# The first feed-forward step's way down as seven block products for eight, and the gate and up sums made by one transfer and three VectorE additions in both steps

## The chip, the cores and the metric

The kernel runs on one core of one Trainium2 chip. The metric is the device time of one execution in microseconds (us), as the median of several runs. TensorE (PE) multiplies, VectorE (DVE) and ScalarE (ACT) do the element-wise work, GpSimd (POOL) and SyncE (SP) issue transfers, POOL also some small copies. Every engine works through its own queue in order; the program that builds the kernel may draw an instruction ahead of its written place if what it needs is there, and fixes the order of each queue before the run.

## The reference

One layer of a decoder stack works on 512 prompt rows and 64 sample rows (8 sequences of 8) with the same weights, 1024 channels wide:

```python
x = x + 0.5 * swiglu(rmsnorm(x, ffn1_norm), ffn1_w_gate, ffn1_w_up, ffn1_w_down)
...  # mixer: RG-LRU heads and pooling heads between w_in and w_out
...  # cross attention over 256 memory rows, 4 heads
x = x + 0.5 * swiglu(rmsnorm(x, ffn2_norm), ffn2_w_gate, ffn2_w_up, ffn2_w_down)
y = rmsnorm(x, final_norm)

def swiglu(x, w_gate, w_up, w_down):
    return (silu(x @ w_gate) * (x @ w_up)) @ w_down
```

The hidden width of a feed-forward step is 2816, that is 22 chunks of 128. All arrays are float32.

## The kernel before

`x` lies transposed in SBUF, channels on partitions: 8 tiles of 128 channels by T = 576 rows, the rows in two halves of HT = 288. Every product is done in fp32r with hi and lo parts: `split` (L188 to L193) makes the hi part with a ScalarE cast and the lo part with a VectorE subtraction, and each block product is three matmuls (hi x hi, hi x lo, lo x hi). A panel of weights therefore costs one cast and one subtraction before TensorE can use it. The tiles of hi and lo parts rotate through WSB = 5 buffers (tags `wh`, `wl`), the raw weights through WRB = 4 (tag `wr`).

Both feed-forward steps are one function, `ffn`; the second is called with `fast=True`.

**Gate and up.** The first chunks (STD: 3 in the first step, 2 in the second) are multiplied plainly. For every further chunk, gate and up weights and the two halves of the rows form a 2 x 2 block product, done as seven block products instead of eight. The products are called by their weight operand: 11, E, F, G, 12, H and 22; each is 4 blocks x 3 matmuls = 12 matmuls of 288 columns. The operands of the activations (`n1`, `n2`) are prepared once; the weights of each chunk have to be summed. E, F, G and H are sums or differences of the four weight blocks.

- First step: `load` brings all four blocks by two SP transfers, and `prepare_a` and `prepare_b` make the sums with four VectorE additions of 128x512 (L472, L473, L474, L485).
- Second step: two of the sums come from HBM. During the first step and the mixer, `background` has POOL copy blocks into a scratch array `gsum` and accumulate the others onto them (L173, L176). `load_pairs` fetches them, and `sum_g` (L509, L510) makes the other two on VectorE. `prepare_e`, `prepare_g`, `prepare_h` and `prepare_22` split the pairs.

**Way down.** Its products are `steps` in a queue; `fill()` puts one of them between two products of a chunk.

- First step: plain. Five groups of chunks (FGS = 4, 4, 4, 5, 5). For each group and each of 8 output panels, `down` multiplies the hidden chunks by the panel's weights (tile `pd`, 6 matmuls a chunk), and VectorE adds the result to `x` (L572). The last group runs after the last chunk, and each finished panel goes straight to the mixer's norm (`after(j)`). The hidden chunks are split as they are made (`hh`, `hl`).
- Second step: chunks 0 to 15 form four groups of four, each again a 2 x 2 block product done as seven (`quick`; tiles `d`). `build_a` and `build_b` make the operands from two hidden chunks with four subtractions and five splits (tiles `ph`, `pl`). `ensure` makes the weight operands of one of the 16 down tiles: two sums from `dsum` in HBM (made by `background` like `gsum`), two by VectorE (L657), four splits. Results go to `x` by accumulating POOL transfers (`take`, then L694, L721, L728). Chunks 16 to 21 (PLAIN) go through `down` in groups of two and four; the last group is the tail with the final norm.

A group of seven products has 6 slots: `s11`, `sE`, `sF`, `s12`, `sH`, and `sG` with `s22`. Each block product here is 2 blocks x 3 matmuls = 6 matmuls.

The order of TensorE's instructions is as written (`chain` in `mm`). The place where `background` may issue is tied to the latest matmul. `first` ties the ScalarE casts that are written after it behind a given instruction.

## Time and profile before

| | |
|---|---|
| median of 3 runs | 1133.25 us (1132.85 to 1133.92) |
| the profiled execution | 1133.87 us, of which the span of its instructions is 1132.1 us |
| TensorE busy | 1118.3 us, 8526 instructions |
| VectorE busy | 833.0 us |
| ScalarE busy | 604.0 us |
| POOL busy | 135.0 us |
| first feed-forward step | about 5 to 399 us |
| mixer and output projection | about 399 to 541 us |
| attention | about 541 to 738 us |
| second feed-forward step with the tail | about 739 us to the end |

The page gives busy time by engine, then the chain of work that ended last, then groups of instructions by source line, operation and tile; a group's row ends with its busy time, the mean duration of one in ns, and the idle time of its engine just before it with what ended that. Matmuls overlap, so a single one shows about 295 ns while one starts every 133 ns. Other views list who waited for whom, the transfers with the median time to landing, and the busy time of all engines in given stretches.

### The profile page before, as it was taken

To read this page: it belongs to the slowest core of one execution; us is meant where nothing else is said; L and a number is where in the kernel's file an instruction comes from. 1 tells how busy PE (TensorE), PEld (TensorE's weight loads), DVE (VectorE), ACT (ScalarE), POOL (GpSimd) and SP (SyncE) were. 2 spreads that over 40 slices of the span, in tenths; PEclk is the share of its full clock that TensorE was granted. 3 is DMA by queue.
4 is the path that set the end of the run, shared out by engine and by line. 5 is a ranking of instruction groups with operands and counts; after the bars stand their busy time and mean duration, and the time that the engine had idled before them with its cause. 6 is when DMAs were issued, how large, how long until landed. Compare 5 with 4: busy or idle time off the path is not lost.

```text
span 1132.1 us, 21308 instructions
## 1 busy us (share of the span) xinstructions
PE 1118.3 (99%) x8526; PEld 1101.1 (97%) x8526; DVE 833.0 (74%) x1391; ACT 604.0 (53%) x1047; POOL 135.0 (12%) x177
## 2 busy tenths in 40 slices
PE   9999999999999999999999999999999999999996
PEld 8999999999999999999999889999999999999996
DVE  8887778787775698977733666669878888787644
ACT  8544444444432454875721455446666666666544
POOL 0011111111111033310000000000121111212111
PEclk9999999999999999999999999999999999999998
DMA  9355766576675388642566762223675766766652
GB/s 317 99 146 153 183 168 160 139 170 174 154 181 113 102 234 184 125 153 86 189 207 215 270 229 79 77 79 94 163 171 150 188 161 163 193 164 157 152 118 84
DMA packets 82547, 179.58 MB, mean 159 GB/s; under 512 B 8272, under 2 KB 28752, under 8 KB 82320
## 3 DMA queue, kind: packets, MB, share of 16 engines
q1 hardware_dynamic: 55728, 129.92, 35.6%
q0 software_dynamic: 24064, 45.88, 22.7%
q10 hardware_dynamic: 2656, 2.41, 0.6%
q8 instruction: 67, 1.10, 0.4%
q14 instruction: 32, 0.26, 0.1%
HBM read 156.86 MB, written 34.17 MB: 169 GB/s over the span
## 4 chain that ended last, share of the span: by engine, by line
PE 93%; DVE 3%; DMA 1%; ACT 1%; issue 1%; SPq 0%; DVEq 0%; ACTq 0%
PE pu L140 22%; PE pd L140 15%; PE pc L140 11%; PE d L140 7%; PE pa L140 5%; PE q L140 5%; PE wo L140 5%; PE xo L140 5%; PE pg L140 2%; PE in_l L140 2%; PE in_p L140 2%; PE in_g L140 2%; PE v L1396 2%; PE k L140 2%; PE o L140 1%; PE s L140 1%
## 5 line engine op out<-in xcount | busy, mean ns | idle before, releaser
L140 PE MATMUL pd<-hh,dh 128*128 128x288 f32 x352 | 75.3, 295 | 0.0
L140 PE MATMUL pd<-hl,dh 128*128 128x288 f32 x352 | 75.0, 294 | 0.0
L140 PE MATMUL pd<-hh,dl 128*128 128x288 f32 x352 | 75.0, 294 | 0.0
L188 ACT CAST wh_e<-r 128x1024 fp32r<-128x1024 f32 x39 | 41.0, 1051 | 57.5 <-PE pu L140 22.8
L140 PE MATMUL d<-ph,dh 128*128 128x288 f32 x224 | 66.6, 297 | 0.2 <-ACT add_e L677 0.2
L140 PE MATMUL d<-ph,dl 128*128 128x288 f32 x224 | 66.0, 295 | 0.0
L140 PE MATMUL d<-pl,dh 128*128 128x288 f32 x224 | 65.8, 294 | 0.0
L694 POOL DMA_DIRECT2D x<-add_e x16 | 19.3, 1204 | 380.8 <-ACT dh L188 348.6
L140 PEld LDWEIGHTS pd<-hl,dh 128*128 128x128 f32 x352 | 56.5, 188 | 0.0
L140 PEld LDWEIGHTS pd<-hh,dh 128*128 128x128 f32 x352 | 56.4, 188 | 0.0
L140 PEld LDWEIGHTS pd<-hh,dl 128*128 128x128 f32 x352 | 56.1, 188 | 0.0
L191 DVE TENSOR_TENSOR wl_e<-r,wh_e 128x1024 fp32r<-128x1024 f32 x39 | 47.7, 1222 | 10.5 <-ACT wh_e L188 10.5
L188 ACT CAST wh_g<-r 128x1024 fp32r<-128x1024 f32 x39 | 41.0, 1052 | 22.1 <-DVE r L485 15.1
L191 DVE TENSOR_TENSOR wl_g<-r,wh_g 128x1024 fp32r<-128x1024 f32 x39 | 47.7, 1223 | 5.2 <-ACT wh_g L188 4.1
L188 ACT CAST dh<-wr_d 128x512 fp32r<-128x512 f32 (+2 forms) x50 | 31.0, 619 | 36.0 <-PE pd L140 14.7
L140 PE MATMUL pu<-n1h,wh_a 128*128 128x288 f32 x152 | 45.0, 296 | 0.0
L140 PE MATMUL pu<-n1h,wl_a 128*128 128x288 f32 x152 | 44.9, 295 | 0.0
L140 PE MATMUL pu<-n1l,wh_a 128*128 128x288 f32 x152 | 44.6, 293 | 0.0
L936 ACT ACTIVATE g<-g 128x576 f32<-128x576 f32 x39 | 26.8, 686 | 32.8 <-DVE g L935 32.6
L140 PEld LDWEIGHTS d<-ph,dh 128*128 128x128 f32 x224 | 42.0, 188 | 0.8 <-ACT add_e L677 0.4
L191 DVE TENSOR_TENSOR dl<-td,dh 128x512 fp32r<-128x512 f32 x48 | 33.1, 690 | 12.6 <-ACT dh L188 10.9
L140 PEld LDWEIGHTS d<-pl,dh 128*128 128x128 f32 x224 | 42.2, 188 | 0.0
(570 smaller groups left out, 4250.1 us busy)
## 6 DMA issues: line engine op xcount, KB each, us to landing
gsum<-f_gu POOLq DMA_DIRECT2D x40, 512.0 KB, 8.5
r<-f_gu SPq DMA_DIRECT2D x38, 512.0 KB, 3.9
r<-f_gu SPq DMA_DIRECT2D x60, 256.0 KB, 3.8
x<-add POOLq DMA_DIRECT2D x40, 288.0 KB, 4.3
r<-gsum SPq DMA_DIRECT2D x40, 256.0 KB, 4.0
dsum<-f_d POOLq DMA_DIRECT2D x32, 256.0 KB, 5.6
ck<-ck SPq DMA_DIRECT2D x16, 512.0 KB, 4.4
cv<-cv SPq DMA_DIRECT2D x16, 512.0 KB, 6.9
```

The costliest lines, as they stand in the source:

```text
L140: i = te.matmul(*args, **kw)
L188: i = cast[0] = s.copy(hi, src)
L191: return v.tensor_tensor(out=lo, in0=src, in1=f(hi), op=ALU.subtract)
L694: nc.gpsimd.dma_start(x[:, j:j + 2, HT:], t, accum_op=ALU.add)
L936: s.activation(g, g, AF.Silu, scale=-1.0)
L1396: te.matmul(ps[:, m, :HD], lhsT=lhs[:, kd, ms], rhs=w[wi][:, k, :], start=kd == 0 and i == 0, stop=kd == DC - 1 and i == 2)
```

## The change

The first step's `ffn` now works like the second: `fast` is gone, and both use `quick`, `ensure`, `build_a`, `build_b` and PLAIN for the way down. In the first step the last group (chunks 18 to 21) is still added to `x` by VectorE, panel by panel, for the mixer's norm. The two sums of down weights that the second step takes from `dsum` are made by VectorE in the first (`ensure`, `elif head`).

In both steps `gsum` is gone. A chunk's blocks come by SP transfers (`load_11`, `load_12`, `load_22`). `sum_eh` makes H by one VectorE addition, and E by a POOL transfer from HBM that accumulates onto the raw block; it is written two chunks ahead of use. `prepare_g` makes the other two sums with two VectorE additions. The splits of H/12 and of G/F are written one product later than before, that of 22 one product earlier. The 32 transfers for `dsum` remain and are now issued in the mixer and the output projection. WRB goes from 4 to 6, WSB from 5 to 4. Small things: the constants `ones` and `eps` share a tile, `neg` keeps two gains, the `half` factor is gone (the 0.5 is applied on the way down), and in the last scaling VectorE's first multiply stands ahead of ScalarE's copy of the row factor.

```diff
-WRB, WSB = 4, 5
+WRB, WSB = 6, 4
...
-    nfast = FFC - STD[1]
-    gsum = [scratch.tile([P, 2, KP * P], F32, name=f"gsum{i}") for i in range(nfast)]
     dsum = [scratch.tile([NQ, P, 2, 2 * P], F32, name=f"dsum{i}") for i in range(FAST)]
...
-        def prepare_a(f):
...
-        def prepare_b(f):
...
-        def load_pairs(f):
+        def load_11(f, behind=None):
             if f < FFC:
...
+                raws[f] = [raw_tile("r0")]
+                i = nc.sync.dma_start(raws[f][0], wgu[f - plain, :, 0:2])
+                if behind is not None:
+                    after_(i, behind)
+
+        def load_12(f, behind=None):
+            if f < FFC:
+                raws[f].append(raw_tile("r1"))
+                i = nc.sync.dma_start(raws[f][1][:, 0], wgu[f - plain, :, 2])
+                if behind is not None:
+                    after_(i, behind)
+
+        def sum_eh(f):
+            if f < FFC:
+                r0, r1 = raws[f]
+                v.tensor_add(r1[:, 1], r0[:, 0], r0[:, 1])
+                nc.gpsimd.dma_start(r0[:, 0], wgu[f - plain, :, 3], accum_op=ALU.add)
...
-        def sum_g(f):
+        def prepare_g(f):
             if f < FFC:
                 r0, r1 = raws[f]
                 v.tensor_add(r0[:, 1], r0[:, 1], r0[:, 0])
                 v.tensor_add(r0[:, 0], r0[:, 1], r1[:, 0])
-
-        def prepare_g(f):
-            if f < FFC:
-                W[f]["G"], W[f]["F"] = parts_of(raws[f][0], "g")
+                W[f]["G"], W[f]["F"] = parts_of(r0, "g")
...
-                if k == fg - 1 and fast:
+                if k == fg - 1 and after:
+                    xj = halves(x[:, j, :])
+                    v.scalar_tensor_tensor(out=xj, in0=pd[j][:, :, :HT], scalar=0.5, in1=xj, op0=ALU.mult, op1=ALU.add)
+                    after(j)
+                elif k == fg - 1:
                     add = rows.tile([P, T], F32, tag="sq", name="add")
                     s.activation(halves(add), pd[j][:, :, :HT], AF.Copy, scale=0.5)
                     nc.gpsimd.dma_start(x[:, j, :], add, accum_op=ALU.add)
...
+        def fetch_pair(i):
...
                     if k:
                         v.tensor_add(t[:, k], t[:, k], t[:, k - 1])
+                    elif head:
+                        v.tensor_add(t[:, 3], t[:, 0], t[:, 1])
+                        v.tensor_add(t[:, 0], t[:, 0], draw[i, 0])
                     split(*w, t[:, k:k + 2])
                     if k == 2:
-                        fetch_main(i + 1)
+                        fetch_pair(i + 1)
...
+        if head:
+            ps2 = accumulators(2)
+            w = panel(wstd[2, 0], DC, P, "s", load_behind=squares_in)
+            load_11(plain, squares_in)
+            load_12(plain, squares_in)
+            sum_eh(plain)
+            std(cols(ps2[0]), w, range(DC))
+            load_22(plain)
+            std_out(1, *ps1)
+            n.sums(3, ts[1][:, 1])
+            w = panel(wstd[2, 1], DC, P, "s")
+            first[0] = spread_out
+            prepare_e(plain)
+            std(cols(ps2[1]), w, range(DC))
+            load_11(plain + 1)
+            load_12(plain + 1)
+            std_out(2, *ps2)
+            prepare_g(plain)
+            first[0] = None
...
             product(U, w["11"], n, N11, True)
             s.copy(A, U)
...
+            if f == plain:
+                if not head:
+                    prepare_g(f)
+                load_11(f + 2)
...
             product(C, w["E"], n, T1, True)
             e1 = small_tile("e1")
             s.copy(e1, C)
-            if fast and f == 3:
+            prepare_h(f)
+            load_12(f + 2)
+            if f == plain:
+                sum_eh(f + 1)
+            if f == 3:
                 build_a(0)
                 build_b(0)
             fill()
             if before:
                 finish_chunk(before)
...
+            prepare_e(f + 1)
             fill()
-            if fast and f in range(4, 4 * FAST + 1, 4):
+            if f in range(4, 4 * FAST + 1, 4):
                 quick(f // 4 - 1)
             product(U, w["F"], n, T2, False)
             u2 = small_tile("u2")
             s.copy(u2, U)
-            if fast:
-                sum_g(f + 1)
+            prepare_22(f)
+            load_22(f + 2)
             fill()
             product(C, w["G"], n, N22, False)
...
+            sum_eh(f + 2)
             fill()
...
             product(A, w["12"], n, N21, False)
...
             fill()
             product(U, w["H"], n, T3, False)
...
+            prepare_g(f + 1)
+            load_11(f + 3)
             raw[f] = g
...
-        s.copy(rb, pr)
-        finish(nc.gpsimd, nc.scalar, c0, c1, 6, 8, rb)
         for i in range(3):
             finish(v, nc.sync, c0, c1, 2 * i, 2 * i + 2, pr)
+            if i == 0:
+                s.copy(rb, pr)
+                finish(nc.gpsimd, nc.scalar, c0, c1, 6, 8, rb)
```

More of the change, by code (lines that the diff above doesn't have):

```diff
@@ L798, in ffn @@
         for i in range(3):
-            i = s.copy(r[:, i * third:(i + 1) * third], free[i][:, HT:HT + third])
-        spread_out = i
-        if fast:
-            half = r
-        else:
-            half = fp.tile([P, T], F32, name=f"half_{n.name}")
-            s.activation(half, r, AF.Copy, scale=0.5)
-        std(cols(ps1[1]), w, range(mid, DC))
-        if not fast:
-            group(0)
-        std_out(0, *ps0)
-        if fast:
-            load_pairs(plain)
+            spread_out = s.copy(r[:, i * third:(i + 1) * third], free[i][:, HT:HT + third])
@@ L839, in ffn @@
[L839 to L857 removed]
+        load_22(plain + 1)
@@ L877, in ffn @@
         for f in range(plain, FFC):
-            if not fast and f - g0 == FGS[gi]:
-                g0, gi = f, gi + 1
-                group(gi)
             w = W[f]
@@ L1515, in hybrid_step @@
                 copy()
+                if h == XH - 2:
+                    first[0] = cast[0]
         sample_values(7)
@@ L1524, in hybrid_step @@
         prompt_values(3)
+        first[0] = None
         end("xa")
@@ L1540, in hybrid_step @@
                 n2.sums(j // 2, now["r1"].tile([P, 3, HT], F32, tag="A", bufs=2, name=f"t_n2{j}"))
+    assert not jobs and not added
     end("r2", "r1", "ps")
```

266 lines of the change are left out of this document (77 added, 189 removed).

## The prediction

> **What bounds the kernel now.** I read the page's busy shares first, then the chain that ended last, then TensorE's own waits over the whole run and over the second feed-forward step, and then the busy time by stretches.
>
> ```profile
> span 1132.1 us, 21308 instructions
> PE 1118.3 (99%) x8526; PEld 1101.1 (97%) x8526; DVE 833.0 (74%) x1391; ACT 604.0 (53%) x1047; POOL 135.0 (12%) x177
> ...
> 364.85 34.39 PE pd L140 x258
> ...
> 840.06 0.80 PE d L140 x6
> 840.86 1.59 PE pc L140 x12
> ...
> 853.56 3.18 PE pu L140 x24
> ...
> PE warm L140 <- POOL ident masks.py:199: 1.4, 1, 1.4
> PE rs L140 <- DVE rf_f L288: 1.3, 1, 1.3
> PE pg L140 <- ACT wh L188: 1.2, 1, 1.2
> ...
> PE d L140 <- ACT add_e L677: 0.2, 1, 0.2
> ```
>
> The last column of the chain rows is the number of matmuls in the piece. TensorE is the bound. Its longest waits are about a microsecond each, at the start and in the tail; inside the second step (764 to 1090 us) it waited once, 0.2 us. A busy PE alone proves little, so the pace is what I use: 34.39 us / 258 = 0.133 us and 3.18 / 24 = 0.1325 us per 288-column matmul, in two places 490 us apart. Nothing but a smaller number of matmuls shortens such a stretch, and anything that makes TensorE wait lengthens it one for one.
>
> ```profile
> 113.00:283.00 170.00, 170.00 (x1288) 170.00 (x1287) 133.67 (x200) 72.08 (x109) 24.00 (x30) 1.00 0.69 166
> 28.30:56.60 28.30, 28.14 (x211) 27.72 (x210) 25.24 (x39) 16.25 (x25) 1.31 (x2) 1.00 0.35 99
> 366.00:396.00 30.00, 30.00 (x227) 30.00 (x226) 20.61 (x28) 14.34 (x21) 0.00 (x0) 1.00 0.36 111
> 765.00:793.00 28.00, 28.00 (x214) 28.00 (x213) 26.17 (x47) 18.55 (x31) 0.00 (x0) 1.00 0.33 95
> 850.00:906.00 56.00, 56.00 (x424) 55.87 (x423) 47.71 (x84) 38.22 (x77) 9.44 (x10) 1.00 0.67 167
> 906.00:962.00 56.00, 56.00 (x424) 55.91 (x423) 45.27 (x80) 36.90 (x74) 10.24 (x11) 1.00 0.68 163
> 962.00:1019.00 57.00, 57.00 (x431) 56.87 (x430) 45.33 (x78) 37.27 (x77) 10.15 (x10) 1.00 0.71 178
> ```
>
> Columns: stretch and its length, then busy PE, weight load, VectorE, ScalarE, POOL, granted clock, DMA share, GB/s. VectorE is the second engine: 79% in the first step's loop, 82% (138.31 of 169) in the second's. At 765 to 793 it was busy for 93% while PE was full.
>
> **The change part by part.**
>
> ```profile
> L140 PE MATMUL pd<-hh,dh 128*128 128x288 f32 x352 | 75.3, 295 | 0.0
> L140 PE MATMUL d<-ph,dh 128*128 128x288 f32 x224 | 66.6, 297 | 0.2 <-ACT add_e L677 0.2
> ```
>
> *Matmuls.* The first step's way down is 3 x 352 = 1056 matmuls (three hi/lo passes; the second and third rows of the group are alike). With the second step's scheme 16 of the 22 chunks go as seven products: 3 x 224 = 672, plus 6 chunks x 8 panels x 2 halves x 3 = 288 for the plain ones: 960. So 96 matmuls go, all on the bounding engine: 96 x 0.1325 = 12.7 us. The 7 x 12 matmuls of each gate/up chunk stay.
>
> A page of the Trainium skill, "TensorE: Matmul & The Clock Gate" (Part 1), would price a warm matmul at N / 2.4 GHz plus 2.5 ns, by estimate 122.5 ns for 288 columns, and so the removal at 11.8 us. The trace has 132.5 ns; I use the trace.
>
> *VectorE.* A chunk's share of PE work in the loop is 84 + 672/16 = 126 matmuls, 16.7 us; VectorE's part of it in the second step is 0.818 x 16.7 = 13.7 us.
>
> ```profile
> L509 DVE TENSOR_TENSOR r<-r 128x512 f32<-128x512 f32 x10 | 6.9, 687 | 0.0
> L657 DVE TENSOR_TENSOR td<-td 128x256 f32<-128x256 f32 x19 | 8.0, 419 | 0.2
> L572 DVE TENSOR_TENSOR x<-pd,x 128x576 f32<-128x576 f32 x19 | 14.3, 752 | 2.1 <-PE pd L140 2.1
> L191 DVE TENSOR_TENSOR wl_e<-r,wh_e 128x1024 fp32r<-128x1024 f32 x10 | 12.2, 1220 | 0.0
> L193 DVE SCALAR_TENSOR_TENSOR pl<-g,ph 128x576 fp32r<-128x576 f32 x5 | 3.8, 754 | 0.0
> L193 DVE SCALAR_TENSOR_TENSOR pl<-g,ph 128x288 fp32r<-128x288 f32 x5 | 2.3, 453 | 0.0
> L188 ACT CAST wh_e<-r 128x1024 fp32r<-128x1024 f32 x10 | 10.5, 1053 | 3.9 <-PE pu L140 3.9
> L694 POOL DMA_DIRECT2D x<-add_e x16 | 19.3, 1204 | 380.8 <-ACT dh L188 348.6 <-ACT add_e L677 32.3
> x<-add POOLq DMA_DIRECT2D x40, 288.0 KB, 4.3
> gsum<-f_gu POOLq DMA_DIRECT2D x40, 512.0 KB, 8.5
> td<-f_d SPq DMA_DIRECT2D x16, 256.0 KB, 4.9
> ```
>
> The second step gains one 128x512 add per chunk (three for two): 0.69, so 14.4 of 16.7 us, 86%. The first step becomes that plus two 128x256 adds per down tile, one tile per chunk (0.84): 15.2 of 16.7, 91%; its 32 additions from PSUM (L572, 0.75 each) go to POOL transfers. Hidden by PE if VectorE can keep 91%; 93% beside a full PE was seen, for 28 us. ScalarE takes over the second step's load (37.27 of 57, 65%) in the first: hidden. I take 0 for the loops; the other end is the first rival.
>
> *The early transfer.* Per chunk, E = W1 + W4 is now a POOL transfer that accumulates into the raw tile, behind a VectorE add that reads the tile first; ScalarE's cast of E/11 (`prepare_e`) waits for it, and on ScalarE the PSUM copies queue behind, for which PE would wait. In the loop `sum_eh(f + 2)` stands after product G of f and the operand is needed at product 11 of f + 2: nine products of 1.59 and about ten fills of 0.8 later, 22 us. The transfer itself is not in the trace. From its nearest row (x<-add, 4.3; far end gsum, 8.5) the chain is 0.69 add + 1.2 issue + 4.3 (8.5) + 1.05 cast + 1.22 subtract = 8.5 us (12.7). Covered.
>
> The exception is the start of the first step, where chunk 3 has no fills:
>
> ```profile
> 48.07 0.29 PE L140 MATMUL pu<-n1h,wh_a 128*128 128x288 f32 x1
> 51.25 0.30 PE L140 MATMUL pu<-n1h,wh_e 128*128 128x288 f32 x1
> ...
> 773.60 0.29 PE L140 MATMUL pa<-n2h,wh_h 128*128 128x288 f32 x1
> ...
> 774.98 1.22 DVE L191 TENSOR_TENSOR wl_h<-r,wh_h 128x1024 fp32r<-128x1024 f32 x1
> ```
>
> `sum_eh(4)` stands behind product E (ends 51.25); product 11 of chunk 4 starts at 48.07 + 6 x 1.59 = 57.6, only 6.4 us later. In written order that would be late by 2.1 us (6.4 with 8.5). But the queues are not in written order: wl_h at 774.98 is chunk 3's, whose place is after its product 11, yet it was made while chunk 2's 12 ran (773.60). If the add is drawn ahead as soon as its tile has landed, nothing is late. VectorE is also loaded here (89% in 28 to 57): ahead of chunk 3 it loses two weight splits of 1.22, five 512-wide sums and splits of 0.69 and two 576-wide splits of 0.75 (7.4 us), gains four 512-wide sums and one split of 1.22 (4.0), and must now build the first pair (seven 288-wide instructions of 0.45 and two 576-wide of 0.75, 4.7 us) before chunk 3's g finds a buffer. Bounds 0 to 6.4 us; nearest the case with look-ahead: I take 0.6.
>
> *Four hi/lo buffers for five.* Each weight split may start about one or two products later.
>
> ```profile
> 783.18 1.21 DVE L191 TENSOR_TENSOR wl_g<-r,wh_g 128x1024 fp32r<-128x1024 f32 x1
> ...
> 792.63 0.29 PE L140 MATMUL pu<-n2h,wh_g 128*128 128x288 f32 x1
> ```
>
> wl_g stood ready at 784.4, 8.2 us before use; two products less leaves 5 us. Cost 0; with that cover gone, the gate/up products would wait first. In the mixer and attention a panel takes 48 matmuls, 6.4 us of PE, against 2.3 us of cast and subtract: 0.
>
> *Queues.* POOL loses 40 gsum transfers and gains 39 E transfers and 56 additions into x; at about 1.2 us each, some four per 16.7 us chunk. An E transfer can stand behind an addition that waits for ScalarE; 22 us cover it. The 32 dsum transfers move into the mixer, where POOL already issued one or two after each projection. SP's down tiles (4.9 us) get one more row of adds; the second step's cadence is kept. All 0. The end of step one: 24 matmuls (3.2 us) a panel for 30, VectorE 20.61/30 x 4 = 2.7 us a panel: hidden. The `half` activation goes from ScalarE: 0. In the last scaling one multiply moves ahead of ScalarE's copy of the factor:
>
> ```profile
> 1125.38 0.38 ACT rb L1041
> ```
>
> so 0.4 us either way, taken as 0.
>
> **Sum.** The profiled execution took 1133.87 us (span 1132.1 and 1.8 around it), 0.6 above the median of 1133.25. 1133.87 - 12.7 + 0.6 = 1121.8; against the median, 1121.2.
>
> **The rivals.**
> *VectorE becomes the bound (slower).* If its in-order waits on ScalarE keep it from more than the 85% (47.71 of 56) that the second step's loop has shown, a first-step chunk takes 15.2/0.852 = 17.8 us for 16.7, 1.1 more over 17 chunks, 19 us, and the second step's 14.4/0.852 = 16.9, 0.2 over 17, 3 us: 1133.25 - 12.7 + 22 = 1143. It decides from where 12.7 us are lost: 0.75 a chunk, a ceiling of 87%. For it: the share is an average, and builds come in lumps. Against it: 93% and 89% beside a full PE. 8%, a quarter of it so close to that ceiling that the time hardly moves.
>
> *The early transfer is late at the start of step one*, by 2.1 to 6.4 us once: 1122.7 to 1127. For it: VectorE is full there. 12%. By the Trainium skill, "SBUF — State Buffer" (SBUF: two separate sides), VectorE can keep POOL from writing descriptors; "DMA: Bandwidth & Descriptors" (Anatomy of one DMA) would instead have 256 KB land in an estimated 2.6 us. No run here shows either; the 4.3 us row already contains both.
>
> *The removed matmuls don't all pay*, because the end of step one is set by the additions and the norm rather than by PE: at 4.0 us a panel as before, 6.4 us of the 12.7 are lost: 1127.6. Against it: 2.7 us. 4%.
>
> **How the numbers follow.** PE-bound as summed: 76%, range 1119.8 (nothing late, 0.4 us at the tail, 0.4 for the pace of 0.133 and the runs' spread) to 1123. With the late transfer and the lost tail the range 1119.6 to 1126.5 leaves out little more than VectorE's bound and the far ends. A difference of 0.2% (2.3 us) is about what can be told here; faster 92%, same 2%, slower 6%.
>
> **What would show it.** Right: about 96 fewer matmul records, the first step's d group like the second's (x224), PE without waits over 0.3 us from 60 to 385 us, VectorE near 90% there and 85% in the second step. Wrong: PE waiting for ACT wh_e (the transfer late), for wl_g, wl_h or pl (VectorE behind), or a pace above 0.133 us. The forecast fails if such waits recur chunk by chunk: 0.33 us in each of 39 chunks undoes it.

## The result, and the profile after

The changed kernel takes 1144.97 us (median; 1144.37 to 1145.84) and the kernel before, on the same chip, 1133.07 (1132.85 to 1133.92): a ratio of 1.0101, 95% interval 1.0089 to 1.0113. It is 11.9 us slower where 12.1 us faster was forecast. The profiled execution's span is 1143.7 us.

From the page of the changed kernel: span, busy times, the chain that ended last, and one group of matmuls (times, mean ns, idle time ahead and what ended it).

```profile
span 1143.7 us, 21674 instructions
PE 1115.2 (98%) x8430; PEld 1091.4 (95%) x8430; DVE 863.1 (75%) x1521; ACT 670.1 (59%) x1246; POOL 191.7 (17%) x232
...
PE 74%; DVE 11%; DMA 6%; issue 4%; ACT 4%; POOL 0%; POOLq 0%; SPq 0%; ACTq 0%; DVEq 0%
...
L139 PE MATMUL d<-ph,dh 128*128 128x288 f32 x448 | 134.9, 301 | 12.9 <-ACT add_e L638 7.9
```

The matmuls fell from 8526 to 8430, 96 as forecast, and the quick way down now has twice 224 in each of the three hi/lo passes. But the chain is TensorE for 74% only, and the new group stood idle for 12.9 us. TensorE's waits, longest sums first (us, times, longest):

```profile
PE d L139 <- ACT add_e L638: 7.9, 8, 1.2
PE d L139 <- ACT d L646: 4.0, 5, 1.0
PE pg L139 <- DVE rf_n L282: 2.7, 1, 2.7
```

Lines 638 and 646 are ScalarE's copies out of the accumulators of the quick way down; rf_n is the row factor at the start of the first step. To place the loss, the table gives, for every kernel of this text, three lengths read from the start times of matmuls: "start" from the first 288-column matmul of step one to the first of its gate/up chunk 3, "loop" from there to the mixer's first matmul, "second" from the second step's first gate/up chunk to the first 256-column matmul of the tail. All three are of the one profiled execution of a kernel, which can differ from the median by some microseconds (e2_start 1140.29 for 1144.76, e14_td2pair 1133.22 for 1138.00). The median is of all executions, the ratio to the kernel before on the same chip. What is left of the span is 0.2 to 1.0 us longer than before in every one of them, 0.9 us in the changed kernel. The last column is VectorE's waiting for the down tile (td and t2) between 54 and 350 us.

| kernel | median us | ratio to before (95%) | start | loop | second | td waits |
|---|---|---|---|---|---|---|
| before | 1133.07 | 1 | 42.59 | 351.01 | 340.44 | - |
| after | 1144.97 | 1.0101 (1.0089-1.0113) | 46.37 | 355.08 | 343.30 | 18.4 |
| e1_pair | 1136.23 | 1.0030 (1.0019-1.0040) | 44.91 | 349.78 | 339.97 | 13.9 |
| e2_start | 1144.76 | 1.0092 (1.0070-1.0113) | 42.59 | 354.44 | 343.21 | 15.9 |
| e3_poolsum | 1145.63 | 1.0104 (1.0089-1.0119) | 47.68 | 353.33 | 344.66 | on POOL |
| e4_noE | 1136.98 | 1.0028 (1.0017-1.0040) | 46.59 | 346.77 | 342.16 | 6.9 |
| e5_notd | 1135.09 | 1.0015 (1.0005-1.0025) | 46.84 | 345.01 | 342.13 | 0 |
| e6_single | 1135.52 | 1.0018 (1.0009-1.0028) | 48.22 | 347.15 | 339.76 | 18.2 |
| e7_lessadd | 1139.18 | 1.0047 (1.0032-1.0062) | 48.43 | 349.11 | 341.33 | 20.3 |
| e8_all | 1136.43 | 1.0026 (1.0015-1.0037) | 44.36 | 353.04 | 340.13 | 22.6 |
| e9_dsum1 | 1145.08 | 1.0091 (1.0068-1.0114) | 47.22 | 356.03 | 343.43 | on ScalarE |
| e10_both | 1141.04 | 1.0063 (1.0044-1.0083) | 42.84 | 359.60 | 339.17 | on ScalarE |
| e11_cut | 1134.82 | 1.0010 (1.0001-1.0019) | 44.47 | 350.83 | 339.70 | 19.2 |
| e12_td2 | 1140.68 | 1.0069 (1.0054-1.0084) | 47.90 | 349.16 | 342.14 | 12.2 |
| e13_td2single | 1132.74 | 0.9996 (0.9987-1.0006) | 49.10 | 344.41 | 338.15 | 15.3 |
| e14_td2pair | 1138.00 | 1.0049 (1.0032-1.0065) | 48.35 | 346.41 | 338.30 | 14.1 |
| e17_pin | 1141.71 | 1.0079 (1.0064-1.0094) | 46.42 | 350.92 | 343.96 | 5.1 |
| **e15_all** | **1120.14** | **0.9888 (0.9871-0.9904)** | 42.23 | 339.08 | 338.15 | 0 |
| e18_double | 1128.66 | 0.9957 (0.9940-0.9974) | 42.93 | 343.30 | 342.16 | 0 |
| e19_nopin | 1125.87 | 0.9931 (0.9916-0.9946) | 43.64 | 343.94 | 338.15 | 14.7 |

So the change lost 3.8 us at the start, lost 4.1 in the loop where 12.7 were to be won, and lost 2.9 in the second step. Within the loop most of it was lost where one group of four gate/up chunks passes into the next: set beside e15_all, the fastest kernel below, the loop is 16.0 us longer, and about 11 of that lie in three pairs of a group's last chunk and the next group's first, 1.7 more in the first group's first. A group has a short chunk, its first (108 matmuls, 14.31 us; the others 126 to 138), because 24 down steps have 28 fills, and three of the four empty ones lie in it. Stretches by window, columns as in the prediction; a chunk is counted here from ScalarE's copy of its product 11 to that of the next chunk. Before, in the second step: a pair made of the last chunk of one group and the first of the next, and the short one of the two alone. Then after: such a pair in the first step, its short chunk, another pair there, a pair in the second step, its short chunk, and most of the loop.

```profile
840.10:871.19 31.09, 31.09 (x236) 31.00 (x235) 25.20 (x45) 20.68 (x42) 4.44 (x5) 1.00 0.73 183
856.78:871.19 14.41, 14.41 (x110) 14.32 (x109) 13.47 (x24) 9.73 (x21) 1.20 (x1) 1.00 0.68 177
```

```profile
115.41:150.70 35.29, 32.29 (x236) 31.12 (x235) 28.85 (x52) 20.42 (x41) 7.09 (x8) 1.00 0.70 154
135.32:150.70 15.38, 13.19 (x96) 12.49 (x95) 14.60 (x26) 9.65 (x20) 2.08 (x2) 1.00 0.73 158
186.69:221.13 34.44, 32.13 (x236) 31.14 (x235) 28.31 (x51) 20.40 (x42) 6.58 (x7) 1.00 0.73 158
917.39:949.40 32.01, 31.23 (x236) 31.00 (x235) 25.79 (x46) 20.60 (x41) 6.18 (x7) 1.00 0.78 179
934.06:949.40 15.34, 14.55 (x110) 14.32 (x109) 13.79 (x24) 9.61 (x20) 2.06 (x2) 1.00 0.73 168
113.00:283.00 170.00, 163.54 (x1209) 160.37 (x1209) 141.46 (x253) 105.42 (x215) 37.78 (x39) 1.00 0.70 155
```

The 234 matmuls of a pair (236 touch the window) took 31.09 us, and now 35.29, 34.44 and 32.01. In the loop VectorE was busy for 141.46 of 170 us, 83%: over the loop it stayed below the 91% reckoned with, and TensorE waited all the same. But the mean hides the short chunk, where it was busy for 14.60 of 15.38 us, more than the 14.31 us that the chunk's matmuls need. Two places of the timeline show how (start, duration, instruction; in brackets the idle time ahead and what ended it). VectorE, and then ScalarE a panel later:

```profile
124.96 0.43 DVE L617 TENSOR_TENSOR td<-td 128x256 f32<-128x256 f32 x1 [3.41 <-DMA td<-f_d]
125.30 0.69 DVE L185 TENSOR_TENSOR wl<-r,wh 128x512 fp32r<-128x512 f32 x1
```

```profile
140.78 0.68 ACT L186 ACTIVATE ph<-g 128x576 fp32r<-128x576 f32 x1 [1.34 <-DVE g L801]
141.37 0.39 ACT L646 COPY d<-d 128x288 f32<-128x288 f32 x1
143.31 1.05 ACT L182 CAST wh_g<-r 128x1024 fp32r<-128x1024 f32 x1 [1.54 <-DVE r L483]
...
144.88 0.71 ACT L638 ACTIVATE add_e<-d 128x288 f32<-128x288 f32 x2
```

VectorE stands 3.41 us at the down tile's first sum, with ready work behind it, just ahead of the short chunk. A late VectorE leaves ScalarE waiting (for g, for r), and behind that wait stand the copies of lines 646 and 638, whose inputs had been ready for 2.0 to 2.4 us; TensorE's next d products wait for them.

### The profile page after: what moved, and what is told of

Same layout as the page of the kernel before. It is cut to its first block, busy times and chain, and to the rows that moved or that the text cites. A ratio compares the mean times of both kernels' runs of the same rounds, so it can differ in the third digit from the quotient of the medians.

```text
span 1143.7 us, 21674 instructions
## 1 busy us (share of the span) xinstructions
PE 1115.2 (98%) x8430; PEld 1091.4 (95%) x8430; DVE 863.1 (75%) x1521; ACT 670.1 (59%) x1246; POOL 191.7 (17%) x232
## 4 chain that ended last, share of the span: by engine, by line
PE 74%; DVE 11%; DMA 6%; issue 4%; ACT 4%; POOL 0%; POOLq 0%; SPq 0%; ACTq 0%; DVEq 0%
PE pu L139 16%; PE d L139 11%; PE pc L139 7%; PE pd L139 5%; PE q L139 5%; PE xo L139 5%; PE wo L139 5%; PE pa L139 3%; DMA td<-f_d 3%; PE pg L139 2%; PE in_l L139 2%; PE in_p L139 2%; PE in_g L139 2%; DMA r<-f_gu 2%; PE v L1318 2%
## 5 line engine op out<-in xcount | busy, mean ns | idle before, releaser
L139 PE MATMUL d<-ph,dh 128*128 128x288 f32 x448 | 134.9, 301 | 12.9 <-ACT add_e L638 7.9
L139 PE MATMUL d<-pl,dh 128*128 128x288 f32 x448 | 132.1, 295 | 0.0
L139 PE MATMUL d<-ph,dl 128*128 128x288 f32 x448 | 131.9, 294 | 0.0
L139 PEld LDWEIGHTS d<-ph,dh 128*128 128x128 f32 x448 | 84.1, 188 | 18.6 <-ACT add_e L638 11.4
L139 PEld LDWEIGHTS d<-ph,dl 128*128 128x128 f32 x448 | 84.3, 188 | 0.0
L139 PEld LDWEIGHTS d<-pl,dh 128*128 128x128 f32 x448 | 84.2, 188 | 0.0
L182 ACT CAST dh<-td 128x512 fp32r<-128x512 f32 x96 | 59.3, 618 | 38.9 <-DVE td L615 18.3
L682 POOL DMA_DIRECT2D x<-add x32 | 28.7, 898 | 208.6 <-ACT add L638 157.8
L182 ACT CAST wh_g<-r 128x1024 fp32r<-128x1024 f32 x39 | 41.0, 1051 | 30.3 <-DVE r L483 14.7
L638 ACT ACTIVATE add<-d 128x288 f32<-128x288 f32 x128 | 52.0, 406 | 7.1 <-PE d L139 7.1
L185 DVE TENSOR_TENSOR wl_h<-r,wh_h 128x1024 fp32r<-128x1024 f32 x39 | 47.6, 1222 | 5.3 <-ACT wh_h L182 5.3
L689 POOL DMA_DIRECT2D x<-add x32 | 33.1, 1036 | 0.0
```

Of the source, the lines that this page charges most:

```text
L139: i = te.matmul(*args, **kw)
L182: i = cast[0] = s.copy(hi, src)
L185: return v.tensor_tensor(out=lo, in0=src, in1=f(hi), op=ALU.subtract)
L638: s.activation(dst, src, AF.Copy, scale=0.5 * sign)
L682: nc.gpsimd.dma_start(x[:, 2 * (i % NQ), :], t, accum_op=ALU.add)
L689: nc.gpsimd.dma_start(x[:, 2 * (i % NQ) + 1, :], t, accum_op=ALU.add)
```

## The experiments

Three theories came from this: a late td stops VectorE; VectorE simply has too much to do in the short chunk; the double PSUM tiles (two accumulators in one tile of two banks) turn ScalarE's small delays into TensorE's. The early transfer and the start were to be told apart from them.

**The double tiles regrouped.** Product E writes C, whose tile also holds U, and so it waits for the copy A<-U, which it doesn't need.

```
-  ps[i] = [t[:, h, :HT] for t in (d0, d1) for h in range(2)]
+  ps[i] = [t[:, h, :HT] for h in range(2) for t in (d0, d1)]
```

> The only edit: the four PSUM accumulators U, C, A, D of the quick way down are put into the two double tiles as (U, A), (C, D) instead of (U, C), (A, D), in both steps. Theory (the losses are made where a short chunk, the first of each group of four with 108 matmuls or 14.3 us, meets 14.6 us of VectorE; a late VectorE holds ScalarE's queue, and the PSUM copies of the quick steps behind it): the product E then no longer waits for the copy A<-U, and the next no longer for the two copies out of C, so the pairs of waits of 0.99 and 1.18 us at d go (4 groups in the first step, one wait of 1.2 us in 3 groups of the second). But VectorE stays as busy, so the wait can come back at the next operand it makes: 1135 to 1143 us, median about 1139, with the short chunks at 14.4 to 15.0 us for 15.4. Rival (VectorE's work alone sets the short chunk, no matter which copy is waited for): no change, 1144 to 1146, the wait at wl_g, wl_h or pl.

1136.23 us, in the theory's range. The second step is whole again (339.97); the loop won 5.3, and what was left moved to the next wrong neighbour:

```profile
PE d L139 <- ACT add L638: 6.7, 8, 1.7
```

**The start.** `after_(q, gate[0])` on the first sum of panel 0, gate[0] being VectorE's last instruction of the first standard chunk.

> The only edit: the sums of the first step's first down tile (td, lines 617 and 618 on VectorE) are ordered behind VectorE's work on the first standard chunk, so they and the splits that follow are not drawn into the chain of the row factor at 26.9 to 33.6 us. Theory (the 2.7 us wait of pg for rf_n at 29.2 us, the granted clock of 0.94 that follows it, and the E transfer issued at 32.1 us behind it, all come from five td instructions drawn ahead): the wait goes, the first gate/up product starts 2.7 to 3.8 us earlier, 1141.2 to 1142.3 us. Rival (the start is late because VectorE has more to do there, 89 per cent before the change, wherever it stands): the work moved comes back as waits between 46 and 64 us, 1144 to 1146 us.

The start is that of the kernel before to the hundredth, 42.59. In the changed kernel VectorE's order there was this; the td and dl rows stand between the steps of the row factor, though they are written at the end of the first gate/up chunk:

```profile
28.63 0.16 DVE L740 TENSOR_SCALAR rf_n<-ms_n 128x5 f32<-128x5 f32 x1
28.73 0.69 DVE L185 TENSOR_TENSOR dl<-td,dh 128x512 fp32r<-128x512 f32 x1
29.34 0.18 DVE L278 RECIPROCAL rf_n<-rf_n 128x5 f32<-128x5 f32 x1
29.45 0.42 DVE L615 TENSOR_TENSOR td<-td 128x256 f32<-128x256 f32 x1
...
31.68 0.16 DVE L282 SCALAR_TENSOR_TENSOR rf_n<-rf_n,rf_n 128x5 f32<-128x5 f32 x1
```

The queues are laid out ahead of the run, each instruction where its inputs are reckoned to be ready; td was. The whole time hardly moved, though (1143.8 to 1146.1 in three executions, 1140.3 in the profiled one), as the rival had it: the work came back as a wait of 3.0 us of TensorE in chunk 3, for a ScalarE copy behind the cast of the down tile. The theory was right about the start and wrong about the total.

**The sums on POOL**, `nc.gpsimd.tensor_add` for `v.tensor_add` in lines 617 and 618.

> The only edit: the two 128x256 sums of each down tile of the first step (lines 617 and 618) run on POOL instead of VectorE: 0.85 us less VectorE work a chunk in the first step, as the second step has it; the second step is unchanged. Theory (VectorE's load in the short chunks): VectorE's part of the short chunk falls from 14.6 to 13.8 us, the second step's value, so the first step's loss there falls from about 3.4 us a group to the second step's 1.05: about 7 to 9 us in all, and with the start freed of two of its instructions up to 1 more: 1135 to 1138 us. Rival (the single td tile and its late transfer hold the queue, not VectorE's load: it waited 18.4 us in 11 waits for td): the sums still come late, the losses stay within 3 us, 1142 to 1145; if POOL is slow at the sums (over 1.5 us each, or behind additions waiting for ScalarE) the splits come later still and it is slower than 1145.

No gain (1145.63; loop 1.75 us shorter), as the rival had it. Less VectorE work alone doesn't mend the first step; the sums still wait for td, now on POOL (22.7 us in 9 waits), and ScalarE's cast for POOL.

**Without the early transfer**, the one `dma_start` of `sum_eh` left out.

> Leaves out the addition of W4 into E: the POOL transfer that accumulates into the raw tile is not issued, in both steps; all else stays (E is then W1 alone). The prediction's step three (the transfer is covered by about 22 us in the loop): no change in the loop, the d waits stay, 1143 to 1145.5 us, with up to 1.9 us at the start, where wh_e waited that long for the transfer. Rival (the transfer is what comes late, ScalarE's cast of E waits for it and the PSUM copies queue behind): the short chunks go from 15.4 to 14.3 us and the time to 1125 to 1135.

1136.98, the loop 8.3 us shorter: far from the theory, just above the rival's range, and by another way than either had. ScalarE's cast of E was not what waited in the loop. What got shorter was the landing of the down tile (last column: median us from issue to landing; after, then without the transfer):

```profile
td<-f_d SPq DMA_DIRECT2D x16, 384.0 KB, 5.0
```

```profile
td<-f_d SPq DMA_DIRECT2D x16, 384.0 KB, 3.7
```

VectorE's waits for td fell from 18.4 to 6.9 us. The second step's td rows got shorter too (256 KB from f_d, 5.5 to 4.3 us), and with them went the 4.8 us that ScalarE had waited for td there. So the early transfer was covered by its own 22 us, and its traffic made another transfer late that had no cover. The Trainium skill, "DMA: Bandwidth & Descriptors" (Issuing engines are not separate DMA queues), says that transfers run on the same 16 DMA engines whichever engine starts them; these two rows agree.

**Without the reload of td** (all panels use the first tile).

> Leaves out the reload of the main down tile (td) after the first panel, in both steps: all panels work on the first panel's tile; the casts, sums, products and the reload of the small tile t2 stay. Theory (the main tile has one buffer, is asked for only after the last split out of it, and lands 5 us later, just when VectorE's two sums want it; VectorE, in order, stood 18.4 us in 11 waits for it between 54 and 350 us, and all its other work behind it): the waits for td go and with them 6 to 12 us of the first step's 16.4 us of excess; the second step, whose first use of the tile is ScalarE's, gains 0 to 2: 1133 to 1139 us. Rival (VectorE's load in the short chunk, 14.6 us for 14.3, sets the loss; waiting for td only fills its idle time): the first step stays within 3 us of 355 us, 1142 to 1145.

1135.09; loop 345.01: without the reload, and so without its traffic as well, the loop is 10.1 us shorter. What remains is 1.0 us in six of the eight short chunks, alike in both steps, 1.4 in the first, and the start.

**Single PSUM tiles**: `bank_`, `[P, 512]`, four buffers, for `dual`, `[P, 2, 512]`, two.

> The double PSUM tiles (two banks) are replaced by single ones (one bank, four buffers), so each of U, C, A, D of the quick way down has a tile of its own, in both steps; where one instruction read both banks, in 6 plain panels' additions and the standard chunks, two now do. Theory (a product waits for ScalarE's last copy out of its double tile, though the copy reads the other half; the regrouping took the second step's waits almost away and left the first step's at 'add'): no product waits for a copy of another accumulator: the second step as before the change (340.0 us from chunk 2 to the tail), the first step's loop 342 to 348 us, total 1127 to 1134. Rival (the regrouping only moved the waits, VectorE and td decide): the first step stays at the 349.8 us of the regrouping or above, 1135 to 1139.

1135.52; second step 339.76 and loop 347.15 as the theory had it, the total just above its range and within the rival's, because the start got worse (48.22): the pause at the row factor was 3.0 us here, and TensorE's granted clock was 0.53 and 0.62 in the two 4 us windows behind it, for 0.66 and 0.91 in the changed kernel. Now `pu` waited for ScalarE's copy of u (4.2 us in 5 waits), and the three pairs of the first step still took 33.3 to 33.5 us for 31.0: the double tiles passed the delays on, they did not make them.

**One VectorE sum fewer**, the second of `prepare_g`.

> Leaves out the second of VectorE's two sums for G and F of each gate and up chunk (128x512, 0.61 us from start to start), in both steps; F then is E. Double tiles as in the changed kernel. Theory of VectorE's load (the second step lost 1.0 us in each short chunk because a third sum took VectorE there from 13.46 to 13.86 us of 14.31): the second step's short chunks return from 15.35 to 14.4, 3 us, and the first step loses some 0.6 to 1 us less in each of its four: 1137 to 1141. Rival (only the late td tile and the double tiles count, VectorE has slack): the second step's short chunks stay at 15.3 and the time at 1143 to 1145.

1139.18, in the theory's range: three short chunks of the second step took 14.3 us for 15.35, though 0.2 to 0.9 us of each loss stayed, now in the chunk ahead. VectorE's amount of work matters there, but for the most part through the double tiles: with single tiles and all three sums (e6_single) that step as a whole is as short as before, though two of its pairs still lose 0.8 and 1.0 us against e15_all.

**Several at once, and the third split earlier** (`ensure(4 * i + 3)` from `sF` to `sE`).

> Three edits together, nothing left out: the single PSUM tiles; the first down tile's sums of the first step ordered behind the first gate and up chunk's own g (so out of the row factor's chain and of the first standard chunks); and the third split of a down tile made one quick step earlier (at product E instead of F), so that the reload of td is asked for about 2.4 us earlier. Theory (the start costs 3.8 us, the double tiles and the late td the rest): start as before (42.6 us to chunk 3), second step 340, first loop 338.5 to 343: 1119 to 1126 us, faster than both kernels. Rival (VectorE's load itself is the limit, 14.6 us in a short chunk of 14.3 and what the start moves into the first two chunks): the loop stays above 346, 1128 to 1136.

The theory failed: 1136.43, loop 353.04. td was asked for earlier, and VectorE waited longer for it, 22.6 us, once 4.45. Asking earlier had moved the sums ahead as well: in e6_single and here alike, from the third tile on, VectorE came to a tile's first sum 2.5 to 5.4 us after the tile was asked for. Six of the microseconds lost lie in the pair of chunks with the wait of 4.45, where TensorE paused for 3.4 us and its granted clock fell to 0.57.

**Other ways of bringing the tile**: sums added in DRAM ahead of time (e9), that with single tiles (e10), the load cut into 256 and 128 KB with single tiles (e11).

> The two outer sums of each down tile of the first step are made as the second step has them: by POOL transfers that add in DRAM ahead of their use (16 more dsum jobs, five started before the first gate and up chunk, then one a chunk), and td is loaded with the sums in it; lines 617 and 618 are gone. Double PSUM tiles as in the changed kernel. Theory (the first step's loss is VectorE, in order, standing 18.4 us for td at its first sum, and 0.85 us more work a chunk; the second step, whose td is first read by ScalarE, loses only 1.0 us in a short chunk): the first step's loop comes down to the second step's loss, 343 to 346 us for 355.1, and nothing of td is drawn into the row factor's chain, so the start returns to 42.6 to 44 us: 1130 to 1135 in all. Rival (late is late: ScalarE's cast of td now waits instead and holds ScalarE's queue, and 0.75 MB more DMA traffic a chunk makes td land later still): the loop at 350 to 356, only the start improves, 1139 to 1143.

> The sums by transfers as in e9_dsum1 and the single PSUM tiles of e6_single together, nothing left out. Theory (late td at VectorE, VectorE's lateness passed on by double tiles, and the start are the whole loss): loop 339 to 341.5 us, second step 340, start 42.6 to 44: 1120 to 1124 us, faster than the kernel before by 9 to 13. Rival (what is left in e6_single, waits of pu for ScalarE's copy of u and of du for add, is VectorE's or ScalarE's load and not td): the loop at 344 to 347, 1126 to 1131.

> Single PSUM tiles; the first step's td loaded by two transfers, 256 KB with the blocks of the first sum and then 128 KB, instead of one of 384 KB; its first tile's sums ordered behind the first gate and up chunk's g, as in e8_all, but the third split left at product F. Theory (a late td at the first sum): the 256 KB land about 1 to 1.5 us earlier than the 384 KB (5.0 us), of 1.7 us that VectorE waits on average: loop 342 to 346, start 42.6 to 44.4, 1125 to 1131 us. Rival (a transfer's landing is set by what else is under way, not its size): VectorE's waits for td stay, loop at 347 or above, 1131 to 1136.

1145.08, 1141.04 and 1134.82: the theory missed three times, and the first two were worse than the rivals' ranges too. With VectorE's sums gone ScalarE's cast waited for td instead (14.2 us in e9_dsum1), and td's parts landed in 5.1 and 5.4 us. These two runs also add transfers to the loop: in e10_both ScalarE waited 11.3 us more for additions into x to land before it could fill their tile again. The cut came out as its rival: VectorE's waits were 19.2 us for 18.2 in e6_single, so the landing was not a matter of size.

**A second td buffer** (4 KB from the raw tiles: r22 in slots of 2 KB, `WRB` 4), with double and with single tiles.

> Nothing left out: td gets a second buffer, in both steps, and is asked for a whole panel (about 17 us) ahead of its first use. Its 4 KB come from the raw tiles: the 2 KB r22 tiles get a tag of their own with two slots, and the 4 KB tag falls from six slots to four, so as many raw tiles are in flight as before. The first step's first loads of r22 and td are ordered behind the last load for the row factor. PSUM tiles stay double. Theory (a late td is about 10 us of the first step's loss; leaving its reload out gave 345.0 us for 355.1, and the double tiles keep 1.0 us in each short chunk): VectorE's waits for td go, loop 344 to 347, second step 342, and the row factor's chain is free of td, start 42.6 to 45: 1130 to 1135. Rival (it was the lighter DMA traffic in the runs without the reload and without the E transfer that helped, not the time of asking): VectorE still waits, loop at 350 to 356, 1138 to 1145.

> The second td buffer of e12_td2, the single PSUM tiles of e6_single, and the first tile's sums ordered behind the first gate and up chunk's g; nothing left out. Theory (late td, the double tiles that pass ScalarE's lateness to TensorE, and the start are all): loop 339 to 342, second step 339.5, start 43 to 44.5: 1120 to 1125 us, faster than the kernel before by 8 to 13. Rival (with td on time VectorE's own 14.6 us in a short chunk of 14.3 shows, as waits of pu for u, and the single tiles' two instructions for one add to it): loop 343 to 346, 1125 to 1130.

1140.68 is in the rival's range, 1132.74 above both; both loops, 349.16 and 344.41, lie nearer the rivals' than the theories'. A third kernel, e14_td2pair, has the second buffer and the double tiles regrouped as in e1_pair; 1121 to 1127 us were expected, by the rival 1128 to 1133. It took 1138.00, above both, with a loop of 346.41 in the rival's range and `d` waiting 4.2 us for ScalarE's copies to `add`. In the first two VectorE still waited 12.2 and 15.3 us for td and t2, most of them about a microsecond. The sums had once more been put where td was reckoned to land. The start was late in all three, 47.9, 49.1 and 48.4, and its row is the early transfer, at last as the second rival of the prediction had it (e13_td2single):

```profile
40.52 1.05 ACT L182 CAST wh_e<-r 128x1024 fp32r<-128x1024 f32 x1 [8.35 <-DMA r<-f_gu]
41.59 1.28 ACT L434 ACT_TABLE_LOAD   x1
```

With the loads of r22 and td moved beside it, E landed 8.9 us after its issue at 31.62; ScalarE's cast stood ahead of the Silu of the first standard chunk, and TensorE waited 4.0 us for that chunk's result. In the changed kernel the same cast waited 1.9 us, and TensorE not at all. Where td's sums had left the row factor's chain, the cast waited longer even with the loads in their old place: 3.5 us in e2_start, with no wait of TensorE, 5.3 in e8_all, with 1.6 us of TensorE's.

**The place of the sums alone.** `v` remembers its last instruction; the first sum of each panel is ordered behind it.

```
+  b = v.i
   q = v.tensor_add(t[:, 3], t[:, 0], t[:, 1])
+  after_(q, b)
```

> The changed kernel with one edit: on VectorE the two sums of each down tile of the first step are ordered behind the VectorE instruction written just before them (at product G of the panel before), so they aren't drawn ahead to where td was reckoned to have landed. One td buffer, double PSUM tiles, the E transfer and all loads as in the changed kernel. Theory (the place of the sums in VectorE's fixed order makes its 18.4 us of waiting for td): the waits fall under 5 us, the first tile's sums leave the row factor's chain (start 42.6), loop 345 to 350 with the 1.0 us of the double tiles in each short chunk: 1131 to 1137. Rival (td lands too late for product 11 in any order): the wait moves to dl and to du's and d's products, loop 353 to 358, 1140 to 1146.

1141.71: above the theory's range and within the rival's. Waits for td 5.1 us, and the short chunks of the second to fourth group lose about 0.27 us for about 3 (14.57 us for 14.31), with the double tiles still there. But the first short chunk lost 6.1: its sums, held back with one buffer only, made TensorE wait 2.7 us, and the granted clock fell to 0.50 behind that pause. The start, expected at 42.6, was 46.42, now by the early transfer: the cast of E waited 4.6 us, TensorE 1.9, and the granted clock was 0.57 in the 4 us behind it.

**All of it**: second buffer, single tiles, sums held in place one quick step earlier, E of the first chunk by VectorE from the raw W4 tile.

> Nothing left out. The second td buffer, the single PSUM tiles, and three new edits for the first step: the two sums of each down tile are ordered on VectorE behind the VectorE instruction written just before them and no earlier, at product H instead of G and 22; the E of the first gate and up chunk is added by VectorE from the raw W4 tile instead of the POOL transfer; the loads of the second r22 and of td wait behind the last load for the row factor. Theory (VectorE's queue is in a fixed order, and the sums stand in it where td was reckoned to have landed, so that any later landing stops all behind it; the start is lost because the cast of E waits 1.9 to 8.4 us for its transfer on ScalarE, ahead of a Silu): no wait of VectorE for td over 0.3 us, start 42.6 to 44, loop 338.5 to 342, second step 338.2: 1119.5 to 1124 us, faster than the kernel before. Rival (VectorE's load in the short chunk, 13.6 to 14.6 us of 14.3, is what is left, and sums held back come late for product 11): waits of du and pu stay, loop 344 to 348, 1126 to 1132.

1120.14 us, ratio 0.9888 (0.9871 to 0.9904): faster than both kernels, with the change's 8430 matmuls and the early transfer in 38 chunks of 39. The same stretches, pair, short chunk, loop:

```profile
109.14:140.15 31.01, 31.01 (x236) 31.01 (x235) 27.20 (x51) 20.40 (x41) 6.44 (x7) 1.00 0.77 169
125.83:140.15 14.32, 14.32 (x110) 14.32 (x109) 13.49 (x26) 9.49 (x20) 2.10 (x2) 1.00 0.70 155
113.00:283.00 170.00, 170.00 (x1286) 170.00 (x1285) 150.98 (x271) 112.96 (x231) 38.17 (x39) 1.00 0.73 161
```

The time is in the theory's range. VectorE does 150.98 of 170 us, 89%, beside a TensorE that doesn't wait once in this stretch.

**What of it is needed**: the double tiles put back, then the sums let go again.

> The kernel of e15_all (1120.1 us) with the double PSUM tiles (U, C), (A, D) put back; nothing left out. Theory (the double tiles pass ScalarE's lateness to TensorE wherever VectorE is near full, in the short chunks): the second step returns to 342 to 343.5 us for 338.15, the first step's loop loses 0.3 to 1.0 us in each of four short chunks: 1125 to 1129 us. Rival (with the sums in place ScalarE is on time and the double tiles cost nothing in the first step): the first loop stays at 339 to 340, only the second step loses 4 us: 1124 to 1125.

> The kernel of e15_all with one edit undone: the sums of the down tiles after the first may be drawn ahead on VectorE again; nothing left out. Theory (their place in VectorE's fixed order made the waits for td): VectorE waits about 10 us for td and t2 again between 54 and 350 us, the first loop at 343 to 345 us as in e13_td2single (344.4): 1123.5 to 1127 us. Rival (with a second buffer, single tiles and the start mended the waits for td are cover that costs nothing): 1119.5 to 1121.5.

1128.66 and 1125.87, both in the theories' ranges. The double tiles cost 8.5 us (7.6 when each is set against the kernel before on its own chip; loop 4.2, second step 4.0), with 1.0 us in each of six short chunks. The drawing ahead of the sums costs 5.7 (4.9 by chip; loop 4.9, start 1.4), 3.8 of the loop's in the one chunk with the longest wait, and with it VectorE's waits for td come back:

```profile
DVE td L630 <- DMA td<-f_d: 12.7, 10, 4.4
```

## Why the prediction was wrong

*Matmuls, -12.7.* Right. 96 went, the pace stayed 0.1325 us, and e15_all is 12.6 us (1132.78 to 1120.14) below the kernel before. That the two agree so closely is partly chance. By the profiled spans it is 13.8 (1132.1 to 1118.3): 11.9 in the loop, where all 96 went, 0.4 at the start, less 0.8 elsewhere, and 2.3 in the second step, which no term of the prediction had.

*VectorE, taken as 0.* The sum of its work was sized about right (89% in e15_all for 91%), and so was the judgement that TensorE can stay full beside it. The step that failed is "hidden by PE if VectorE can keep 91%". It took an average over chunks (126 matmuls, 16.7 us, where the short chunk has 108, 14.3 us), and it took hiding for a matter of share alone. In the short chunk the second step's VectorE had 13.47 us of 14.31 before, and 13.79 with one sum more: that lost 0.9 to 2.0 us in three pairs of chunks, through a ScalarE copy that came too late for a product that didn't need it. The double tiles stood in the code the prediction describes; no row of it was asked what a product waits for when ScalarE is a microsecond late.

*Queues, "the second step's cadence is kept, all 0".* This step failed too. td has one buffer, is asked for three quick steps before its use, and had a landing of 4.9 us in the second step; there ScalarE read it first. In the first step VectorE reads it first, and stopped for 18.4 us in 11 waits. e5_notd puts the reload at 10.1 us of the loop, and e17_pin, which only holds the sums in their place, mends three of its four short chunks. Taken alone in the changed kernel, single tiles win as much (e6_single: 7.9 in the loop, 3.5 in the second step), so neither failed step can be called the larger.

*The early transfer.* Covered in the loop, as said, and it landed in 5.2 us for 4.3 reckoned, inside the bounds of 4.3 to 8.5. By the Trainium skill's estimate it would have been 2.6 us ("DMA: Bandwidth & Descriptors", Anatomy of one DMA); the measured row doesn't agree. What was missed is what its traffic did to td: 8.3 us of the loop.

```profile
r<-f_gu POOLq DMA_DIRECT2D x39, 256.0 KB, 5.2
```

*The start, 0.6.* It cost 3.8, and by td's instructions in the row factor's chain (e2_start, 42.59). The prediction counted that the look-ahead would draw the E sum forward in its favour, and not that it would draw the down tile's too.

*Four hi/lo buffers, the end of step one, the tail*: 0 holds to within a microsecond. With four buffers e15_all's TensorE doesn't wait in the loop, and the stages outside the three lengths are 0.8 us longer than before; what in them grew wasn't looked into.

*The rivals.* The first named a ceiling of VectorE near 85% and gave 1143 us; the time came close, the mechanism did not: there is no such ceiling (89% beside a full TensorE). The second, a late E at the start, cost the changed kernel no wait of TensorE. In kernels whose row factor was on time it came at times: not in e2_start, 1.6 and 1.9 us of TensorE in e8_all and e17_pin, and 3.7 to 4.3 us where other loads were moved beside it (e12_td2, e13_td2single, e14_td2pair). e15_all, which makes the first E on VectorE, has no such wait. By the Trainium skill's rule on SBUF's two sides, named there, VectorE could have kept POOL's transfer back; no run here shows that apart. The signs named for "wrong", TensorE waiting for wh_e, wl_g, wl_h or pl, were not the ones that came: it waited for PSUM copies and once for the row factor, in a few places of 0.4 to 2.7 us rather than chunk by chunk.

The whole difference between the changed kernel and e15_all, 24.8 us, is 16.0 in the loop, 5.2 in the second step and 4.1 at the start (profiled executions: 25.4). In the loop the parts overlap: taken alone in the changed kernel, the reload of td is worth 10.1 and the double tiles 7.9; once the rest is mended, drawing ahead is worth 4.9 and the double tiles 4.2. How the loss divides between them in the changed kernel itself is not settled.

## What to carry to other kernels

Ask of each in-order engine what stands at the head of its queue when a transfer is late, not how busy it is: a load's first reader should not be the engine with the least slack, and an instruction drawn ahead to a reckoned landing needs to be held at its written place. Look for the shortest period of the loop, not the mean, and for tiles that join unrelated values in one dependency. A transfer that is well covered still slows those beside it that are not.

## What was not expected of the hardware

In this kernel a pause of TensorE could cost more than half as much again behind it. After the 2.7 us at 29.2 us the granted clock (third column from the right) fell; the changed kernel, 4 us windows after the pause:

```profile
32.00:36.00 4.00, 4.00 (x21) 3.76 (x22) 3.03 (x5) 2.22 (x5) 1.01 (x1) 0.66 0.74 157
36.00:40.00 4.00, 4.00 (x30) 4.00 (x29) 2.98 (x5) 2.88 (x3) 0.00 (x0) 0.91 0.56 179
```

A full window shows 32 matmuls (30 start in it), so these two are 13 short. By start times the first matmul behind the pause came 2.4 us later than in the kernel before, and the 25th and all that follow 3.9: 1.5 us were lost behind the pause. It doesn't always come: 1.9 us in e9_dsum1 (0.50), 1.9 us in e17_pin (0.57) and 2.0 us in e10_both (0.62) brought it, 2.0 us in e1_pair and 3.0 us in e2_start did not; the pauses of about 1.2 us in the changed kernel's loop left it at 1.00. Some kernels with such pauses spread more from execution to execution (e1_pair 1134.4 to 1140.2, e2_start 1140.3 to 1146.1) than e15_all (1119.5 to 1120.7), but the changed kernel hardly does (1144.4 to 1145.8); that the clock is the reason is not shown. The Trainium skill, "TensorE: Matmul & The Clock Gate" (Part 1), has the clock halve after an idle window of about 3.4 us, on a window that runs freely: the free window fits that equal pauses differ, but here pauses well under 3.4 us were enough.
